# A one-element activation ahead of the second load in a cross-entropy kernel

## The chip, the cores and the metric

The kernel runs on one core of a Trainium2 chip. The metric is the device time of one execution in microseconds, lower is better. Before the change it is 85.4 us, the median of three runs (85.2 to 85.45).

## The reference

The input is `logits`, 256 rows of 32000 float32 (32.8 MB), and one label for each row. What is computed for each row is the cross-entropy with smoothed labels:

```python
log_probs = logits - np.max(logits, axis=-1, keepdims=True)
log_probs = log_probs - np.log(np.sum(np.exp(log_probs), axis=-1, keepdims=True))
smooth_targets = np.full((batch, num_classes), smoothing / num_classes)
for i, label in enumerate(labels):
    smooth_targets[i, label] = 1.0 - smoothing + smoothing / num_classes
return (-np.sum(smooth_targets * log_probs, axis=-1)).astype(np.float32)
```

Written out, a row's result is log(sum of exp(x)) minus c_small times (sum of x, plus c_big/c_small times x at the label), with c_small = smoothing / 32000 and c_big = 1 - smoothing. So each logit is read once, and goes into two sums: a sum of exponentials and a plain sum.

## The kernel before

**Layout.** The 256 rows lie as two rows (r = 0 and r = 1) on each of 128 partitions, so a partition has 64000 columns in a line, and the kernel walks along them in tiles. `WIDTHS` gives the tile widths. Row 0 has four tiles of 8000 columns. Row 1 has one of 8000, one of 6272, and then eight that become smaller: 4736, 3648, 2688, 2048, 1536, 1216, 1024 and 832.

**Buffers.** `load` (its transfers are at L166, L167 and L169 in the profile) takes the destination of a tile. Tiles of at least `RING_MIN` = 6000 columns, six in all, share a ring of three buffers and are called `xt` in the profile; a fourth can be loaded only when the first is no longer read. The eight smaller ones have a buffer each, in the pool `tail`, and are called `xl` in the profile. The names R0 to R5 and T2 to T9 in the prediction are these ring and tail tiles in the order of the columns.

**Work on a tile.** A tile is cut into pieces of at most 4032 columns: two for the six ring tiles and the first tail tile, one for the others. On each piece VectorE (DVE) adds its two halves and accumulates the sum (`sum_logits`, L175, output `jd`), and ScalarE (ACT) takes the exponential and accumulates it (`sum_exps`, L187, output `ja`). Both read the same tile, and neither needs the other.

**The rest.** GpSimd (POOL) loads the labels, computes flat indices and gathers the logit at each label (L103 to L123), and scales it into the first column of the plain sums (L146). When a row is complete, `finish` takes the logarithm of the exponential sum on ACT (L193 or L195), turns both results from a column into a row with two transposes on TensorE (L197, L201), and DVE combines them (L202). For row 1 the partial sums of the last tiles are added step by step in `done` (L268, L271, L276), so that little is left when the last tile has been read. One transfer writes the output (L280).

**What sets the order.** A scheduler, which works when the program is built, decides the order in which each engine and each queue issues, and it derives the waits from which instruction writes and which reads a tile. Within a queue or an engine, an instruction that waits holds up all that come after it. Every transfer of logits goes out on the queue of SyncE (SP), but for the second half of the first tile, which goes out on ACT's. The first transfers of both queues are then moved ahead of the program's opening barrier by `_issue_first_transfers_at_start`. ACT's table set (with Exp, Ln and Copy) is loaded once, at L90.

Of the kernel before, what the change touches and what calls it, by code (L numbers as in the profile page):

```python
# [8 lines left out]
FP32 = mybir.dt.float32  # L9
# [3 lines left out]
AF = mybir.ActivationFunctionType  # L13
# [3 lines left out]
WIDTHS = (  # L17
    (8000, 8000, 8000, 8000),
    (8000, 6272, 4736, 3648, 2688, 2048, 1536, 1216, 1024, 832),
)  # L20
# [37 lines left out]
def kernel(  # L58
# [7 lines left out]
    nc = tc.nc  # L66
    nc.at_finalize(_issue_first_transfers_at_start)
    B, C = logits.shape
    P = nc.NUM_PARTITIONS
# [12 lines left out]
    small = ctx.enter_context(tc.tile_pool(name="small", bufs=1))  # L82
# [6 lines left out]
    if tbl is not None:  # L89
        nc.scalar.add_instruction(  # L90
            mybir.InstLoadActFuncSet(
                name=nc.get_next_instruction_name(),
# [6 lines left out]

    x = logits.rearrange("(p r) c -> p (r c)", r=R)  # L100

    lab = small.tile([P, 2 * R], I32, name="lab", tag="lab")
    nc.gpsimd.dma_start(  # L103
        out=lab[:], in_=labels.bitcast(I32).rearrange("(p f) -> p f", p=P)
    )
    rowoff = small.tile([P, R], I32, name="rowoff", tag="rowoff")
    for r in range(R):
        nc.gpsimd.iota(
            out=rowoff[:, r : r + 1],
# [6 lines left out]
        out=flat_idx[:],  # L116
# [5 lines left out]
    for r in range(R):  # L122
        nc.gpsimd.indirect_dma_start(  # L123
            out=gat[:, r : r + 1],
            out_offset=None,
            in_=logits[:],
# [15 lines left out]
    for r in range(R):  # L142
# [4 lines left out]
            out=xsum[:, 0:1],  # L147
# [10 lines left out]
    def load(w: int, col: int, name: str):  # L158
        if w >= RING_MIN:
            xt = ring.tile([P, max(WIDTHS[0])], FP32, name="xt", tag="xt")  # L160
        else:
            xt = tail.tile([P, w], FP32, name=name, tag=name)
        if col == 0:

            h = w // 2
            nc.sync.dma_start(out=xt[:, :h], in_=x[:, :h])  # L166
            nc.scalar.dma_start(out=xt[:, h:w], in_=x[:, h:w])  # L167
        else:
            nc.sync.dma_start(out=xt[:, :w], in_=x[:, col : col + w])  # L169
        return xt  # L170
# [40 lines left out]
    col = 0  # L211
    for r in range(R - 1):
        at = 0
        for t, w in enumerate(WIDTHS[r]):
            xt = load(w, col, f"xl{r}_{t}")
            col += w
            k = pieces[r][t]
            for i in range(k):
                xp = xt[:, i * (w // k) : (i + 1) * (w // k)]
                sum_logits(xp, w // k, xsums[r][:, at + 1 : at + 2])  # L220
                sum_exps(xp, w // k, esums[r][:, at : at + 1])
                at += 1
        both = small.tile([P, 2], FP32, name=f"both{r}", tag=f"both{r}")
        nc.vector.tensor_reduce(  # L224
            out=both[:, 0:1], in_=xsums[r][:], axis=AX.X, op=ALU.add
        )
        nc.vector.tensor_reduce(  # L227
            out=both[:, 1:2], in_=esums[r][:], axis=AX.X, op=ALU.add
        )
        finish(r, both[:, 0:1], both[:, 1:2], None)  # L230
# [14 lines left out]
    for t, w in enumerate(WIDTHS[r]):  # L245
        left = n - 1 - t
        xt = load(w, col, f"xl{r}_{t}")
        col += w
        k = pieces[r][t]
# [16 lines left out]
        if left == 2:  # L266
            with tc.issue_after(part.ins):
                nc.vector.tensor_reduce(  # L268
                    out=done[0][:, 0:1], in_=xsum[:, : at + 1], axis=AX.X, op=ALU.add
                )  # L270
                nc.vector.tensor_reduce(  # L271
                    out=done[0][:, 1:2], in_=esum[:, : at - 1], axis=AX.X, op=ALU.add
                )
        elif left < 2:
            i = 1 - left
            nc.vector.tensor_tensor(  # L276
                out=done[i + 1][:], in0=done[i][:], in1=pairs[i][:], op=ALU.add
# [3 lines left out]
        out=out.rearrange("(g i) -> g i", g=1), in_=res[:].rearrange("g p r -> g (p r)")  # L281
# [36 lines left out]
```

The softmax here doesn't subtract the row's maximum and nothing guards it: scores larger than these inputs give would overflow.

## Time and profile before

| | before |
|---|---|
| median of three runs | 85.4 us |
| the profiled execution | 85.33 us |
| its span | 83.5 us |
| busy: ACT | 59.9 us (72%) |
| busy: DVE | 38.7 us (46%) |
| busy: POOL, PE | 4.2 and 1.5 us |
| moved by DMA | 32.78 MB, mean 392 GB/s |
| ACT idle before an `xt` tile | 19.3 us |
| DVE idle before an `xt` tile, an `xl` tile | 31.3 and 6.8 us |

The span runs from the first instruction of the program to the last one in the profile; the execution's time is 1.83 us more than that. The busy times are sums over stages that differ, so the stage has to be looked up before a number of this table is put to use. A transfer to the ring that is issued while others are queued takes a median of 21.6 us from issue to landing, most of it in the queue.

### The profile page before, as it was taken

Reading aid. Unit: us, or ns where it says so; the run is one execution under the profiler, and the core shown is the slowest. Engines: PE = TensorE matmul, PEld = TensorE weight load, DVE = VectorE, ACT = ScalarE, POOL = GpSimd, SP = SyncE. Lnnn points to the kernel's source line nnn. Section 1 sums busy time; section 2 is a strip of 40 time slices with the busy share of each in tenths; the row PEclk is TensorE's granted clock in tenths of the full one; section 3 lists DMA queues with packets and bytes.
Section 4 is the critical chain, followed back from the end, with each engine's and each line's share of the span. In section 5 each row is a group of like instructions: output and inputs, shape, how many; then the busy total and the mean of one; then the engine's idle time right before and its main releaser. Section 6 shows DMA issues by size and latency. Waiting matters only on the chain.

```text
span 83.5 us, 217 instructions
## 1 busy us (share of the span) xinstructions
PE 1.5 (2%) x4; PEld 0.3 (0%) x4; DVE 38.7 (46%) x52; ACT 59.9 (72%) x45; POOL 4.2 (5%) x14
## 2 busy tenths in 40 slices
PE   0000000000000000000001010000000000000030
PEld 0000000000000000000000000000000000000000
DVE  0000049600596009910497119913936654756660
ACT  5000049990599809993499909998999999999940
POOL 4201630011000000000000000000000000000000
DMA  5999998998899889998999899999999999999400
GB/s 130 421 422 429 421 506 368 491 460 383 383 490 490 383 352 490 490 398 352 475 490 414 352 419 480 456 396 426 426 392 433 418 422 415 409 411 410 182 4 0
DMA packets 2259, 32.78 MB, mean 392 GB/s; under 512 B 337, under 2 KB 338, under 8 KB 850
## 3 DMA queue, kind: packets, MB, share of 16 engines
q1 hardware_dynamic: 2018, 30.72, 87.0%
q10 hardware_dynamic: 144, 2.05, 5.7%
q0 software_dynamic: 96, 0.00, 0.1%
q14 instruction: 1, 0.01, 0.0%
HBM read 32.77 MB, written 0.00 MB: 392 GB/s over the span
## 4 chain that ended last, share of the span: by engine, by line
DMA 59%; ACT 34%; DVE 2%; issue 1%; PE 0%; SPq 0%; DVEq 0%; ACTq 0%
DMA xt<-in_logits_dram 59%; ACT ja L187 34%; DVE jd L175 1%; PE lin_t L197 0%; DVE done L276 0%; SPq L169 0%; DVE lin_row L199 0%; DVE res L202 0%; ACTq L187 0%; DVEq L202 0%; DVEq L276 0%
## 5 line engine op out<-in xcount | busy, mean ns | idle before, releaser
L187 ACT ACTIVATE ja<-xt 128x4000 bf16<-128x4000 f32 (+1 forms) x12 | 40.9, 3409 | 19.3 <-DMA xt<-in_logits_dram 19.3
L175 DVE SCALAR_TENSOR_TENSOR jd<-xt 128x2000 f32<-128x2000 f32 (+1 forms) x12 | 26.0, 2167 | 31.5 <-DMA xt<-in_logits_dram 31.3
L187 ACT ACTIVATE ja<-xl 128x2368 bf16<-128x2368 f32 (+7 forms) x9 | 16.5, 1839 | 0.0
L175 DVE SCALAR_TENSOR_TENSOR jd<-xl 128x1184 f32<-128x1184 f32 (+7 forms) x9 | 10.7, 1184 | 7.0 <-DMA xl<-in_logits_dram 6.8
L187 ACT ACTIVATION_READ_ACCUMULATOR ja<-xt 128x1 f32 x12 | 2.2, 187 | 0.0
L123 POOL DMA_INDIRECT gat<-in_logits_dram,flat_idx x2 | 2.0, 1002 | 0.7 <-POOL ident masks.py:199 0.4
L90 ACT ACT_TABLE_LOAD x1 | 1.3, 1283 | 0.9 <-PEq L299 0.9
L187 ACT ACTIVATION_READ_ACCUMULATOR ja<-xl 128x1 f32 x9 | 1.6, 182 | 0.0
L197 PE MATMUL lin_t<-ident,both 128*1 128x128 f32 x1 | 0.4, 371 | 45.6 <-DVE both L224 45.6
L175 DVE DVE_READ_ACCUMULATOR jd<-xt 128x1 f32 x12 | 1.0, 82 | 0.0
L199 DVE COPY lin_row<-lin_t 1x128 f32<-1x128 f32 x2 | 0.6, 278 | 0.9 <-PE lin_t L197 0.9
L197 PE MATMUL lin_t<-ident,done 128*1 128x128 f32 x1 | 0.4, 372 | 31.5 <-DVE done L276 31.5
L202 DVE SCALAR_TENSOR_TENSOR res<-lin_row,lse_t 1x128 f32<-1x128 f32 x2 | 0.6, 276 | 0.8 <-PE lse_t L201 0.7
L227 DVE TENSOR_REDUCE both<-esum 128x1 f32<-128x8 f32 x1 | 0.2, 164 | 1.6 <-ACT ja L187 1.6
L146 POOL TENSOR_SCALAR xsum<-gat 128x1 f32<-128x1 f32 x2 | 0.4, 222 | 7.9 <-DMA gat<-in_logits_dram,flat_idx 7.9
L103 POOL DMA_DIRECT2D lab<-in_labels_dram x1 | 0.8, 753 | 1.0 <-POOLq L299 1.0
L201 PE MATMUL lse_t<-ident,lse 128*1 128x128 f32 x2 | 0.7, 372 | 2.4 <-ACT lse L193 2.4
L175 DVE DVE_READ_ACCUMULATOR jd<-xl 128x1 f32 x9 | 0.7, 82 | 0.0
L276 DVE TENSOR_TENSOR done<-done,pair 128x2 f32<-128x2 f32 x2 | 0.3, 162 | 0.6 <-ACT ja L187 0.5
L115 POOL TENSOR_TENSOR flat_idx<-rowoff,lab 128x2 int32<-128x2 int32 x1 | 0.2, 195 | 5.4 <-DMA lab<-in_labels_dram 5.4
L195 ACT ACTIVATE lse<-elast,done 128x1 f32<-128x1 f32 x1 | 0.3, 261 | 0.2 <-DVE done L276 0.2
L193 ACT ACTIVATE lse<-both 128x1 f32<-128x1 f32 x1 | 0.2, 202 | 0.2 <-DVE both L227 0.2
(13 smaller groups left out, 2.0 us busy)
## 6 DMA issues: line engine op xcount, KB each, us to landing
xt<-in_logits_dram SPq DMA_DIRECT2D x4, 4000.0 KB, 21.6
xt<-in_logits_dram SPq DMA_DIRECT2D x1, 3136.0 KB, 19.2
xl<-in_logits_dram SPq DMA_DIRECT2D x1, 2368.0 KB
xt<-in_logits_dram SPq DMA_DIRECT2D x1, 2000.0 KB, 11.5
xt<-in_logits_dram ACTq DMA_DIRECT2D x1, 2000.0 KB, 13.1
xl<-in_logits_dram SPq DMA_DIRECT2D x1, 1824.0 KB, 28.3
xl<-in_logits_dram SPq DMA_DIRECT2D x1, 1344.0 KB, 31.1
xl<-in_logits_dram SPq DMA_DIRECT2D x1, 1024.0 KB, 33.1
```

What stands on the lines that cost most here:

```text
L90: nc.scalar.add_instruction(mybir.InstLoadActFuncSet(name=nc.get_next_instruction_name(), act_func_set_id=tbl, ins=[], outs=[],))
L103: nc.gpsimd.dma_start(out=lab[:], in_=labels.bitcast(I32).rearrange("(p f) -> p f", p=P))
L123: nc.gpsimd.indirect_dma_start(out=gat[:, r : r + 1], out_offset=None, in_=logits[:], in_offset=bass.IndirectOffsetOnAxis(ap=flat_idx[:, r ...
L146: nc.gpsimd.tensor_scalar(out=xsum[:, 0:1], in0=gat[:, r : r + 1], scalar1=label_weight, scalar2=None, op0=ALU.mult,)
L175: return nc.vector.scalar_tensor_tensor(out=jd[:, :h], in0=xp[:, :h], scalar=1.0, in1=xp[:, h:w], op0=ALU.mult, op1=ALU.add, accum_out=out,)
L187: nc.scalar.activation(out=ja[:, :w], in_=xp, func=AF.Exp, accum_out=out)
L195: nc.scalar.activation(out=lse[:], in_=se, func=AF.Ln, bias=se_rest)
L197: nc.tensor.transpose(out=lin_t[:], in_=lin, identity=ident[:])
L199: nc.vector.tensor_copy(out=lin_row[:], in_=lin_t[:])
L201: nc.tensor.transpose(out=lse_t[:], in_=lse[:], identity=ident[:])
L202: nc.vector.scalar_tensor_tensor(out=res[:, :, r : r + 1], in0=lin_row[:], scalar=-c_small, in1=lse_t[:], op0=ALU.mult, op1=ALU.add,)
L276: nc.vector.tensor_tensor(out=done[i + 1][:], in0=done[i][:], in1=pairs[i][:], op=ALU.add)
```

## The change

A tile `zero` of one column is set to 0 by DVE at the start. In `load`, ahead of the transfer of the second tile (`col == 8000`), ACT copies `zero` into the first column of that tile's buffer. The transfer then overwrites the column, so it has to wait for the copy; the copy stands behind the load of the tables on ACT. The transfer of the first tile, in two halves on two queues, is as it was. Nothing else in the source changes; line numbers after the edit are 3, and then 7, higher.

```diff
@@ -99,6 +99,9 @@
 
     x = logits.rearrange("(p r) c -> p (r c)", r=R)
 
+    zero = small.tile([P, 1], FP32, name="zero", tag="zero")
+    nc.vector.memset(zero[:], 0.0)
+
     lab = small.tile([P, 2 * R], I32, name="lab", tag="lab")
     nc.gpsimd.dma_start(
         out=lab[:], in_=labels.bitcast(I32).rearrange("(p f) -> p f", p=P)
@@ -160,6 +163,10 @@
             xt = ring.tile([P, max(WIDTHS[0])], FP32, name="xt", tag="xt")
         else:
             xt = tail.tile([P, w], FP32, name=name, tag=name)
+        if col == WIDTHS[0][0]:
+
+
+            nc.scalar.activation(out=xt[:, 0:1], in_=zero[:], func=AF.Copy)
         if col == 0:
 
             h = w // 2
```

## The prediction

> **What bounds the kernel now.** I read the slices of the page first, then the chain that ended last, then the instructions in order of time.
>
> ```profile
> DMA  5999998998899889998999899999999999999400
> DMA 59%; ACT 34%; DVE 2%; issue 1%; PE 0%; SPq 0%; DVEq 0%; ACTq 0%
> ```
>
> The first line is the share of the DMA engines in 40 slices of 2.09 us: full from the second to the 37th. The second is the chain by engine: DMA first, then ACT. The chain in order of time (start, us, what) says when it changes hands:
>
> ```profile
> 1.29 29.89 DMA xt<-in_logits_dram
> 31.27 7.16 ACT ja L187 x4
> 38.45 19.17 DMA xt<-in_logits_dram
> 57.70 5.60 ACT ja L187 x3
> 63.35 4.33 ACT ja L187 x3
> 67.72 3.19 ACT ja L187
> ```
>
> Until 57.7 us transfers set the time; ACT's 7.16 us on a ring tile sit on this chain only because a buffer's release starts the next transfer. From 57.70, when the last ring tile (6272 columns, call it R5) has landed, ACT runs without a hole to the end. The timeline (start, us, engine, line, operation; idle before it in brackets):
>
> ```profile
> 0.91 1.28 ACT L90 ACT_TABLE_LOAD   x1 [0.91 <-PEq L299]
> 0.92 1.09 SPq L169 DMA_DIRECT2D xt<-in_logits_dram  x2
> ...
> 11.50 3.54 ACT L187 ACTIVATE ja<-xt 128x4000 bf16<-128x4000 f32 x1 [9.31 <-DMA xt<-in_logits_dram]
> ...
> 21.73 3.54 ACT L187 ACTIVATE ja<-xt 128x4000 bf16<-128x4000 f32 x1 [3.07 <-DMA xt<-in_logits_dram]
> ...
> 57.70 2.82 ACT L187 ACTIVATE ja<-xt 128x3136 bf16<-128x3136 f32 x1 [0.31 <-DMA xt<-in_logits_dram]
> ...
> 63.36 1.39 DVE L175 SCALAR_TENSOR_TENSOR jd<-xl 128x1184 f32<-128x1184 f32 x1 [2.01 <-DMA xl<-in_logits_dram]
> ...
> 79.97 0.15 ACT L187 ACTIVATION_READ_ACCUMULATOR ja<-xl 128x1 f32 x1
> 80.06 0.16 DVE L276 TENSOR_TENSOR done<-done,pair 128x2 f32<-128x2 f32 x1
> ...
> 80.32 0.26 ACT L195 ACTIVATE lse<-elast,done 128x1 f32<-128x1 f32 x1 [0.20 <-DVE done L276]
> ...
> 81.38 0.32 SPq L280 DMA_DIRECT2D out_dram<-res  x1
> ```
>
> Two facts to take from these lines. From 57.70 to 80.12 (79.97 + 0.15) is 22.4 us of ACT work that cannot start earlier than R5. And the first tail tile (4736 columns, call it T2), next in the queue behind R5, lands at about 63.34, since DVE was waiting for it and started at 63.36.
>
> **What the Trainium skill says.** "DMA: Bandwidth & Descriptors", section "Queues, rings and completion order": on each DMA engine a queue's descriptors are consumed in ring order, though completion is not strictly first in, first out. The trace agrees on the order: two 4.1 MB transfers issued together at 0.92 let their readers go at 21.73 and 31.27, one after the other. "Specifications" of that page gives a fabric ceiling of 435 GB/s; the windows of this trace show 427 to 435 GB/s in the ring stage. "Perfetto Trace Analysis", section "Tensor Engine Instruction (MATMUL, LD_WEIGHTS)", calls ACT and DVE strict FIFO: ACT will not take a tile that has landed while an earlier instruction waits. Here ACT indeed sat 9.31, 3.07, 2.40, 2.33 and 1.91 us before ring tiles.
>
> **The change, part by part.** I compared the order in which both built programs issue. ACT, DVE and POOL keep the order of their tile work (two 128-row reductions of `done` move by a place near DVE's end); SP's queue does not:
>
> ```
> before  R0 first half | R1 R2 R3 R4 R5 T2 T3 ... T9 out
> after   R0 first half | T2 R1(waits for ACT) R2 R3 R4 R5 T3 ... T9 out
> ```
>
> (R0 to R5 are the ring tiles of 8000, 8000, 8000, 8000, 8000 and 6272 columns, T2 to T9 the tail; the second half of R0 goes from ACT's queue as before.) The new ACT copy writes into R1, so R1's transfer now has a writer to wait for. T2 has a buffer of its own and waits for nothing, and the scheduler puts it into the free place. So the second transfer issued is not held at all; it is a tile that is wanted only after all six ring tiles.
>
> *Memset on DVE (128x1).* Nearest row: 0.16 us (the 128x1 reductions). DVE is idle until 11.50. Zero; uncovered, 0.16.
>
> *Copy on ACT (128x1).* Nearest row: the 128x1 ACTIVATE of L193, 0.20 us. ACT is idle from 2.19 to 11.50 waiting for R0. "ScalarE: Activation LUTs", section "What ACT_TABLE_LOAD costs", gives about 1.28 us for the load (the trace: 1.28) plus about 1.38 us of drain, which this trace does not show. So the copy ends between 2.19 + 0.2 + 0.1 = 2.5 and 3.9 us. Queued behind it on ACT is R0's first exponential, waiting until 11.50 anyway. Zero; uncovered, 0.2 to 1.7.
>
> *The hold on R1.* Behind it on SP wait R2 to R5, T3 to T9 and the output. R1 is issued at 2.5 to 3.9 us instead of 0.92. At that time the queues hold R0 (4.1 MB) and T2 (2.42 MB). R0 and R1 before let the reader go at 21.73; T2 has 3264 columns fewer than R1, 1.67 MB or 3.9 us at 430 GB/s, so R0 and T2 keep the DMA engines busy until some 17.8 us, less what lies between the last byte and the landing, which the trace does not split off. The hold has a margin of 12 us or so. Zero; from about 15 us on it would cost 1 us for each.
>
> *T2 ahead of R1 to R5.* 128 x 4736 x 4 bytes = 2.425 MB, carried before all ring tiles but the first. The price can be read without a rate: after the change R5 ends at the same count of bytes at which T2 ended before, so it lands when T2 landed: 63.34 instead of 57.66, **+5.68 us**. With the rate of the ring stage (431 GB/s) it is 2.425 / 0.431 = 5.63. I take 5.66. Does a ring buffer starve on the way? R3 waits for R0's buffer (18.68, unchanged; T2 and R1, R2 are in the queue until about 37). R4 waits for R1's, free at 21.73 + 5.66 + 7.1 = 34.5, with R2 and R3 queued until 46.4; R5 is issued at 44 with R3, R4 queued until 56. The queue never runs dry, so the shift neither grows nor shrinks.
>
> ACT does not use the early T2: its instruction stays behind R5's two. So ACT waits 5.66 us longer for R1, then again follows the transfers at 9.5 us a tile, with 7.2 us of work each, and begins its 22.4 us on R5 at 57.70 + 5.66 = 63.36. Before, those 22.4 us lay beside the tail's transfers with almost no slack on either side; now T3 to T9 land at their old times (67.7 to 79.0, same byte counts) while ACT needs T3 only at 73.4. The cover is lost on the transfer side and nothing is gained on ACT's.
>
> *What comes back at the end.* ACT and DVE now never wait for the tail. Between tiles ACT's steps from one accumulator read to the next start are 0.09 to 0.16 us in the tail against 0.09 within a tile, 0.23 more in all: between 0 and 0.23 comes back, I take 0.1. And the last logarithm at 80.32 waited for DVE's `done` (80.06 + 0.16), which hung on the late sum of T9; now DVE is ahead, and it can start some 0.06 after ACT's end at 80.12: 0.12 comes back. The transposes and the output (2.1 us from 81.38) stay.
>
> *Semaphores of SP.* T5 waits for T2's landing, T8, T9 and the output now wait for the landing of R3, R4 and R5 (before: T7, T8, T9 for R3, R4, R5). T9 goes out by about 56, when over 20 us of transfers are queued. Zero.
>
> **Sum**: 5.66 - 0.10 - 0.12 = +5.44. Span 83.5 + 5.44 = 88.9; the profiled execution's 85.33 becomes 90.77. The median of the runs, 85.4, lies 0.07 above that execution, so 90.8.
>
> **Rivals.**
>
> *The early T2 costs nothing, time stays at 85.4.* This needs R5 to land by 57.7 although 2.425 MB more lie ahead of it: the DMA engines would have to carry 26.1 MB (51008 columns) instead of 23.7 in the 56.4 us from 1.29, 463 instead of 420 GB/s on average. Single slices of the page show 490 and 506, but each has a neighbour at 352 to 383; over whole tiles the windows give 427 to 435, at the page's ceiling. It decides from about 460 GB/s on. Chance 2%, and in it a lucky version that is faster: under 1%.
>
> *The issue order is not what fixes the order of landing*: packets of T2 and of the ring tiles are mixed so that T2 is served last. Then R1 lands at 21.7, the copy and hold are hidden and the time is 85.3 to 85.5. It speaks against it that the ring tiles landed strictly in the order issued. 2%.
>
> *The hold is long.* If the wait of R1 lasted past some 15 us, transfers would stop, and every us would come on top: 92 and more. The table load ended at 2.19 and nothing behind it waits for data. 2%.
>
> *ACT gains back more.* If ACT's steps shorten once the transfers are over (its last 5 us now run beside none), the increase could be 4.9 instead of 5.4: 90.2. The 4000-column exponentials last 3.52 to 3.54 us throughout, which speaks against more than some tenths. This lies in the main case's spread.
>
> **How the numbers follow.** Main case, slower by 5.4: 94%. Its own spread: 5.63 to 5.68 on the transfers, 0 to 0.35 back at the end, some 0.25 of scatter between runs (85.2 to 85.45) and the rate's own: 90.1 to 91.4. The other cases hold 6% and need not be reached. Slower: main case and long hold, 96%; same (within 0.3%, about what this kernel's measurement can tell): 3%; faster 1%.
>
> **What would show it.** In the profile after: SP's first issue past the barrier is a transfer to `xl`; ACT's second ring tile starts at about 27.4 instead of 21.7, and its idle time for `xt` grows from 19.3 to about 25; the first 3136-column exponential starts near 63.4; DVE's waits for `xl` (6.8 us) vanish, DMA slices are full to the same 78 us, and then ACT runs alone for about 6 us. The step on the hold is wrong if the DMA slices show a hole before 17 us; the step on R5 is wrong if it starts much off 63.4; the end is wrong if ACT's stretch from R5 to the last accumulator read is not 22.2 to 22.4 us.

## The result and the profile after

The changed kernel takes 90.38 us (median of six runs, 90.26 to 90.91) against 85.39 us before (six runs, 85.2 to 85.56). The ratio is 1.0594, with a 95% interval of 1.0565 to 1.0623: slower by 4.99 us. The prediction was 90.8, with 90.1 to 91.4 as its range.

The timeline of the kernel after (start, us, engine, line, operation; in brackets the idle time before it and what ended it), at the places that were shown of before:

```profile
0.91 1.28 ACT L90 ACT_TABLE_LOAD   x1 [0.91 <-PEq L306]
0.92 0.33 SPq L176 DMA_DIRECT2D xl<-in_logits_dram  x1
...
2.21 0.20 ACT L169 ACTIVATE xt<-zero 128x1 f32<-128x1 f32 x1
...
2.44 41.91 SPq L176 DMA_DIRECT2D xt<-in_logits_dram  x5
...
11.41 3.54 ACT L194 ACTIVATE ja<-xt 128x4000 bf16<-128x4000 f32 x1 [9.00 <-DMA xt<-in_logits_dram]
...
27.36 3.54 ACT L194 ACTIVATE ja<-xt 128x4000 bf16<-128x4000 f32 x1 [8.80 <-DMA xt<-in_logits_dram]
...
63.28 2.82 ACT L194 ACTIVATE ja<-xt 128x3136 bf16<-128x3136 f32 x1 [0.31 <-DMA xt<-in_logits_dram]
...
68.89 2.16 ACT L194 ACTIVATE ja<-xl 128x2368 bf16<-128x2368 f32 x1
...
85.25 0.15 ACT L194 ACTIVATION_READ_ACCUMULATOR ja<-xl 128x1 f32 x1
85.43 0.26 ACT L202 ACTIVATE lse<-elast,done 128x1 f32<-128x1 f32 x1
...
86.46 0.32 SPq L287 DMA_DIRECT2D out_dram<-res  x1
```

The first transfer past the barrier is one to `xl`, T2, issued at 0.92 and held by nothing. R1 goes out at 2.44, as soon as the copy is done. ACT's second tile starts at 27.36, which was 21.73 before, and R5 at 63.28, which was 57.70. From there ACT again works without a hole up to the last logarithm. T2 took 16.9 us from issue to landing, by the page's list of DMA issues (KB, us), so it lay ready from 17.8 us on. ACT, idle for 8.80 us until 27.36, took it only at 68.89, behind R5:

```profile
xl<-in_logits_dram SPq DMA_DIRECT2D x1, 2368.0 KB, 16.9
```

The windows of the kernel after (stretch, length, then the busy time of PE, PEld, DVE, ACT and POOL, the clock, the DMA share and GB/s) show what has become of the overlap at the end:

```profile
63.30:69.00 5.70, 0.00 (x0) 0.00 (x0) 5.60 (x7) 5.70 (x5) 0.00 (x0) 1.00 0.99 421
69.00:78.00 9.00, 0.00 (x0) 0.00 (x0) 7.59 (x14) 9.00 (x7) 0.00 (x0) 1.00 1.00 410
78.00:86.00 8.00, 0.63 (x2) 0.16 (x2) 1.97 (x8) 7.66 (x13) 0.00 (x0) 1.00 0.04 14
```

The windows of the kernel before, at the same end:

```profile
63.40:78.00 14.60, 0.00 (x0) 0.00 (x0) 9.63 (x16) 14.60 (x15) 0.00 (x0) 1.00 1.00 416
78.00:81.00 3.00, 0.72 (x2) 0.16 (x2) 1.81 (x7) 2.38 (x7) 0.00 (x0) 1.00 0.09 34
```

Transfers run to about 78 us at 410 to 421 GB/s, as before (416). Then they are over, and ACT still has 7.66 us of work where it had 2.38 before: the difference lay beside transfers before. The waits, in total, turn round in the same way:

```profile
ACT ja L194 <- DMA xt<-in_logits_dram: 24.7, 6, 9.0
DVE jd L182 <- DMA xl<-in_logits_dram: 1.1, 2, 0.6
```

ACT's wait for ring tiles was 19.3 us and is now 24.7; DVE's for tail tiles was 6.8 and is now 1.1. One view of this profile misleads. The page's chain by engine reads:

```profile
DMA 72%; ACT 14%; issue 8%; SPq 2%; PE 0%; DVE 0%; ACTq 0%
```

That looks as if transfers bound the kernel more than before (59%). But from 63.28 on ACT is the bound, as the windows show. The same chain in order of time (start, us, what) shows where it goes astray:

```profile
45.81 29.36 DMA xl<-in_logits_dram
...
75.21 1.14 issue
76.35 0.38 ACT ja L194 x2
76.73 2.05 issue
```

It steps from ACT to the landing of a tail tile that ACT had not been waiting for, and books a part of ACT's exponentials as "issue". A chain is to be checked against the busy time of the stage.

### The profile page after: what moved, and what is told of

Its sections match the earlier page's. It is cut to its first block, busy times and chain, and to the rows that moved or that the text cites. A ratio compares the mean times of both kernels' runs of the same rounds, so it can differ in the third digit from the quotient of the medians.

```text
span 88.5 us, 221 instructions
## 1 busy us (share of the span) xinstructions
PE 1.5 (2%) x4; PEld 0.3 (0%) x4; DVE 38.9 (44%) x53; ACT 59.8 (68%) x46; POOL 4.3 (5%) x14
## 4 chain that ended last, share of the span: by engine, by line
DMA 72%; ACT 14%; issue 8%; SPq 2%; PE 0%; DVE 0%; ACTq 0%
DMA xt<-in_logits_dram 38%; DMA xl<-in_logits_dram 33%; ACT ja L194 12%; SPq L176 2%; ACT L90 1%; PE lse_t L208 0%; DVE res L209 0%; ACT lse L202 0%; ACT xt L169 0%; ACTq L194 0%
## 5 line engine op out<-in xcount | busy, mean ns | idle before, releaser
L194 ACT ACTIVATE ja<-xt 128x4000 bf16<-128x4000 f32 (+1 forms) x12 | 40.9, 3409 | 24.7 <-DMA xt<-in_logits_dram 24.7
L194 ACT ACTIVATE ja<-xl 128x2368 bf16<-128x2368 f32 (+7 forms) x9 | 16.4, 1829 | 0.0
## 6 DMA issues: line engine op xcount, KB each, us to landing
xl<-in_logits_dram SPq DMA_DIRECT2D x1, 2368.0 KB, 16.9
```

The lines of the kernel that those rows point to most:

```text
L194: nc.scalar.activation(out=ja[:, :w], in_=xp, func=AF.Exp, accum_out=out)
```

## The experiments

Theory O: what costs is the order, T2's bytes ahead of five ring tiles while ACT's instruction for T2 stays behind them, and the hold is covered by what is queued. Rival H: the hold, the copy or the memset cost the time. The table sums up all runs; the second column is when SP's queue issued R1, the third when ACT started R5, the fourth from there to the start of the last logarithm. The times are medians; of the kernel before the median was 85.28 to 85.39 beside each.

| kernel | R1 issued | R5 on ACT | from R5 to the last log | time, us | ratio to before, 95% |
|---|---|---|---|---|---|
| before | 0.92 | 57.70 | 22.62 | 85.39 | |
| after | 2.44 | 63.28 | 22.15 | 90.38 | 1.0565 to 1.0623 |
| hold, tail in place | 2.44 | 57.58 | 22.44 | 84.99 | 0.9954 to 0.9978 |
| T2 first, no hold | 1.30 | 63.28 | 22.15 | 90.46 | 1.0591 to 1.0624 |
| T2 first and used early | 2.44 | 63.36 | 17.83 | 86.09 | 1.0079 to 1.0109 |
| T5 first, no hold | 1.30 | 60.14 | 22.26 | 87.32 | 1.0227 to 1.0261 |
| T2 and T3 first, no hold | 2.16 | 67.65 | 22.15 | 94.81 | 1.1095 to 1.1138 |
| T2 first, hold to 16 | 16.08 | 63.97 | 22.14 | 90.93 | 1.0638 to 1.0707 |
| T2 first, hold to 19 | 18.65 | 66.76 | 22.14 | 93.73 | 1.0956 to 1.1001 |
| hold to 19, tail in place | 18.83 | 66.78 | 22.44 | 93.96 | 1.0984 to 1.1030 |
| memset only | 0.92 | 57.64 | 22.45 | 85.08 | 0.9965 to 0.9983 |
| memset and copy, no hold | 0.92 | 57.74 | 22.45 | 85.02 | 0.9953 to 0.9973 |
| hold, tail in place, again | 2.44 | 57.77 | 22.44 | 85.00 | 0.9950 to 0.9975 |

### The hold without the order

The changed kernel, with each transfer on SP's queue tied behind the one before it in the source (an edge for the order of issue, with no wait), so that T2 goes back to its place.

```diff
-            nc.sync.dma_start(out=xt[:, :w], in_=x[:, col : col + w])
+            if last_load:
+                with tc.issue_after(last_load[-1].ins):
+                    d = nc.sync.dma_start(out=xt[:, :w], in_=x[:, col : col + w])
+            else:
+                d = nc.sync.dma_start(out=xt[:, :w], in_=x[:, col : col + w])
+            last_load.append(d)
```

> The memset, the copy on ACT and the hold on R1 are kept; the transfers on SP's queue are put back into the order of the columns (R1 to R5, then T2 to T9). Theory O (the order costs, the hold is covered): the hold until 2.44 us lies under R0's 4.1 MB, which keep the DMA engines busy until about 11 us, so R5 starts on ACT at 57.7 again and the time is that of before, 85.4 within 0.3%. Rival H (the wait, the copy or the memset cost something of their own): above 86, up to the 90.4 of the changed kernel.

Measured: 84.99 us. SP's queue and the start of R5 in the timeline of this kernel:

```profile
2.44 0.33 SPq L182 DMA_DIRECT2D xt<-in_logits_dram  x1
...
57.58 2.82 ACT L201 ACTIVATE ja<-xt 128x3136 bf16<-128x3136 f32 x1 [0.30 <-DMA xt<-in_logits_dram]
```

R1 is held until 2.44 as in the changed kernel, and R5 starts at 57.58. The hold, the memset and the copy cost nothing; the whole loss has gone with the order. The time is even 0.34% below that of before (0.22 to 0.46%), which theory O did not expect; the last experiment follows that up.

### The order without the hold

The kernel before, with T2's transfer issued ahead of R1's; the edges of the first experiment, left out below, keep this order on SP's queue. There is no memset, copy or hold.

```diff
+            if t == 1:
+                for e in EARLY:  # (2,)
+                    ahead[e] = load(
+                        WIDTHS[1][e], WIDTHS_0 + sum(WIDTHS[1][:e]), f"xl1_{e}"
+                    )
             xt = load(w, col, f"xl{r}_{t}")
```

> The kernel before, without memset, copy or hold; only T2's transfer is issued ahead of R1's. Theory O: all of the loss, 90.4 (90.2 to 90.6), R5 on ACT at 63.3. Rival H: 85.4, or at most a part of the 5 us.

Measured: 90.46 us. SP's queue and the start of R5 in the timeline of this kernel:

```profile
0.92 0.33 SPq L177 DMA_DIRECT2D xl<-in_logits_dram  x1
1.30 43.06 SPq L175 DMA_DIRECT2D xt<-in_logits_dram  x5
...
63.28 2.82 ACT L196 ACTIVATE ja<-xt 128x3136 bf16<-128x3136 f32 x1 [0.30 <-DMA xt<-in_logits_dram]
```

R1 leaves at 1.30 instead of 2.44, and R5 starts at 63.28 all the same. The order makes all of the loss, and the two runs together decide for theory O.

### T2 first, and used when it lands

The changed kernel with the hold; DVE's and ACT's work on T2 is put right behind that on R0. The edges, and the lines that skip T2 at its old place, are left out below; `load(...)` is shortened.

```diff
+            if t == 0:
+                for e in EARLY:  # (2,)
+                    ahead[e] = load(...)
+                    k, c = pieces[1][e], sum(pieces[1][:e])
+                    h = WIDTHS[1][e] // k
+                    for i in range(k):
+                        xp = ahead[e][:, i * h : (i + 1) * h]
+                        sum_logits(xp, h, xsums[1][:, c + i + 1 : c + i + 2])
+                        sum_exps(xp, h, esums[1][:, c + i : c + i + 1])
```

> The changed kernel (hold kept, T2 first), but the sums and exponentials of T2 stand right behind R0's on DVE and ACT instead of behind R5's. Theory O with ACT in order: R5 still lands at 63.3, but ACT's 4.33 us on T2 now lie between 18.5 and 27.4, where it had been idle for 8.8 us; from R5 on it has 22.12 - 4.33 = 17.8 us of work and no wait for T3 to T9 (each lands before its turn), so it ends at 81.1 and the execution takes 85.39 + 0.7 = 86.1. Rival T (what costs is that the ring tiles land late, whatever ACT does meanwhile): 90.4, as in the changed kernel.

Measured: 86.09 us. ACT in the timeline of this kernel:

```profile
18.52 2.16 ACT L203 ACTIVATE ja<-xl 128x2368 bf16<-128x2368 f32 x1
...
20.68 2.16 ACT L203 ACTIVATE ja<-xl 128x2368 bf16<-128x2368 f32 x1
...
27.44 3.54 ACT L203 ACTIVATE ja<-xt 128x4000 bf16<-128x4000 f32 x1 [4.50 <-DMA xt<-in_logits_dram]
...
63.36 2.82 ACT L203 ACTIVATE ja<-xt 128x3136 bf16<-128x3136 f32 x1 [0.31 <-DMA xt<-in_logits_dram]
...
81.19 0.26 ACT L211 ACTIVATE lse<-elast,done 128x1 f32<-128x1 f32 x1
```

R5 is as late as in the changed kernel, at 63.36, and yet 4.29 us of the loss are back. ACT did T2's 4.33 us in a wait before R1, which shrank from 8.80 to 4.50, and they are gone from the stretch after R5 (17.83 us instead of 22.15). What is left over before, 0.8 us (86.09 against 85.29 beside it), is the lateness that this doesn't make up: R5 starts 5.66 us later, and the stretch after it is 4.79 us shorter. So most of the cost isn't that the ring tiles are late, but that the work for the early bytes stays behind them in ACT's order.

### More or fewer bytes ahead

The kernel before with other tail tiles ahead of R1, again without a hold: T5 alone (`EARLY = (5,)`), then T2 and T3 (`EARLY = (2, 3)`), in the manner of the second experiment.

> The kernel before without a hold, with a smaller tail tile, T5 (2048 columns, 1.05 MB), ahead of R1. Theory O: the shift is that of the bytes, 1.049 MB / 0.431 MB per us = 2.43 us, less the 0.45 us that came back at the end in the changed kernel: 87.4. Rival S (what costs is one transfer out of order, not its bytes): 90.4.

> The kernel before without a hold, with T2 and T3 (8384 columns, 4.29 MB) ahead of R1. Theory O: the bytes give 4.293 / 0.431 = 9.96 us, less 0.45: 94.9, R5 on ACT at 67.7. Rival (the cost levels off, since the ring's three buffers or ACT's spare time take up a part of a longer delay): below 94.

Measured: 87.32 and 94.81 us. The start of R5 with T5 ahead, and with T2 and T3 ahead:

```profile
60.14 2.82 ACT L196 ACTIVATE ja<-xt 128x3136 bf16<-128x3136 f32 x1 [0.30 <-DMA xt<-in_logits_dram]
```

```profile
67.65 2.82 ACT L196 ACTIVATE ja<-xt 128x3136 bf16<-128x3136 f32 x1 [0.30 <-DMA xt<-in_logits_dram]
```

Against 57.70 the shifts are 2.44, 5.58 (T2) and 9.95 us for 1.049, 2.425 and 4.293 MB: 0.430, 0.435 and 0.431 MB per us. R5's delay is that of the bytes, in a straight line from 1 to 4 MB, whether one or two transfers carry them. The whole time grows by 0.4 to 0.5 us less (by 2.03, 5.17 and 9.47 us), because the stretch after R5 is shorter than before, as the table shows.

### How long a hold is covered

T2 first, by the edges of the first two experiments. In one kernel the copy into R1 is made by DVE behind both of R0's sums, in another by ACT behind both of R0's exponentials; a third has the latter hold with the tail in its place. The edit of the second:

```diff
-            nc.scalar.activation(out=xt[:, 0:1], in_=zero[:], func=AF.Copy)
+            with tc.issue_after(exps[-1].ins):  # R0's second exponential
+                nc.scalar.activation(out=xt[:, 0:1], in_=zero[:], func=AF.Copy)
```

> T2 first and the hold on R1 made longer: the copy is made by DVE behind both of R0's sums, so R1 is issued at about 16.2 us instead of 2.44. The prediction put the point from which the hold costs at about 15 us. R0 and T2 are 6.5 MB; at 0.27 MB until 2.1 us and 0.43 MB per us from there they last until 16.7, and from an issue to the first byte some 1.1 us pass (the first issue at 0.0 and the half-filled first DMA slice), so a hole of about 0.6 us: 91.0 (90.5 to 91.4). If the hold is not covered by what is queued, the cost is 13.8 us: over 100.

> T2 first and the hold longer still: ACT's copy stands behind R0's two exponentials, R1 is issued at about 18.8 us. The queue is dry from 16.7 to about 19.9: a hole of 3.2 us in the DMA slices, R5 on ACT at 66.5, 93.6 (93.2 to 94.0).

> The same long hold (R1 at about 18.8 us) with the tail in its place, so only R0's 4.1 MB are queued, which last until about 11.0. A hole of 8.9 us: 94.3 (93.7 to 94.7), 0.7 above the kernel with the same hold and T2 first although no byte is out of order: then T2 is worth as cover what it costs as order. Rival (a hold costs the same whatever is queued): 3.2 us above before, 88.6.

Measured: 90.93, 93.73 and 93.96 us. Of each, SP's issue of R1 and the start of R5. T2 first, the hold to 16:

```profile
16.08 28.95 SPq L185 DMA_DIRECT2D xt<-in_logits_dram  x5
...
63.97 2.82 ACT L208 ACTIVATE ja<-xt 128x3136 bf16<-128x3136 f32 x1 [0.31 <-DMA xt<-in_logits_dram]
```

T2 first, the hold to 19:

```profile
18.65 29.12 SPq L185 DMA_DIRECT2D xt<-in_logits_dram  x5
...
66.76 2.82 ACT L207 ACTIVATE ja<-xt 128x3136 bf16<-128x3136 f32 x1 [0.30 <-DMA xt<-in_logits_dram]
```

The hold to 19 with the tail in place, with the DMA share of its page (40 slices of 2.31 us) ahead:

```profile
DMA  7899800078999999999999999899999999999800
...
18.83 0.33 SPq L185 DMA_DIRECT2D xt<-in_logits_dram  x1
...
66.78 2.82 ACT L205 ACTIVATE ja<-xt 128x3136 bf16<-128x3136 f32 x1 [0.30 <-DMA xt<-in_logits_dram]
```

If each further us of hold delays R5 by one us, the time of issue less the delay of R5 is the moment up to which a hold is free. (Between the two holds with T2 first, 2.57 us of hold cost 2.79.) With R0 and T2 queued the delays against 63.28 are 0.69 and 3.48: free up to 16.08 - 0.69 = 15.4 and 18.65 - 3.48 = 15.2 us. With R0 alone the delay against 57.70 is 9.08: free up to 9.75 us. The two differ by 5.5 us, T2's bytes once more. With R0 alone there was one hold only, so its 9.75 rests on that one-to-one price. The zeros in the slices are the hole itself. SP issued nothing between 0.40 and 18.83 us, though T2 to T9 did not depend on the copy: within its queue the held R1 kept all of them back. The hold to 19 costs about the same with and without T2 in front (66.76 and 66.78): there T2 fills a hole that the hold had torn. The two totals differ by 0.23 us and not by the expected 0.7. The expectation for the tail in place was 0.3 too high, mostly because it started from 85.4; with the memset in the kernel that base is 85.0.

### Why the hold alone is a little faster than before

Three kernels, measured on one chip: the memset alone, the memset and ACT's copy into a tile of its own, and the hold with the tail in place again.

```diff
+    zero = small.tile([P, 1], FP32, name="zero", tag="zero")
+    nc.vector.memset(zero[:], 0.0)
+
+    spare = small.tile([P, 1], FP32, name="spare", tag="spare")  # second kernel only
+    nc.scalar.activation(out=spare[:], in_=zero[:], func=AF.Copy)
```

> Why is the kernel with the hold and the tail in place 0.3 us faster than before? Its profile shows two parts: R5 starts 0.12 us sooner, and the first step of `done` no longer sits 0.52 us idle behind the sum of T8, so the last logarithm starts 0.17 us sooner after ACT's end. This kernel is the kernel before with the memset alone: no copy, no hold. Theory D (one more instruction on DVE's list removes the idle time before `done`, whatever its cause; nothing to do with the hold): 85.1, no idle time before the first step of `done`. Theory X (the hold on R1 itself gains): 85.3, as before.

> The kernel before with the memset and with ACT's copy into a tile of its own: both instructions of the change, no hold. Theory D: 85.1. Theory X: 85.3. If the copy and not the memset brings the gain: 85.0 here and 85.3 with the memset alone.

> The kernel with the hold and the tail in place once more, so that it stands beside the two others on the same chip: 85.0 if the gain is there at all; 85.3 if it was that chip's. Theory X says it is 0.3 below the two others, theory D at most 0.15.

Measured: 85.08, 85.02 and 85.00 us, with 85.28 for before; the intervals of the three ratios overlap, and the hold adds nothing to the memset that can be told. So the gain is not the hold's: theory D. The second kernel shows one thing more: with both new instructions, but no dependence of R1 on the copy, R1 goes out at 0.92 and T2 stays in its place. It is the dependence that moved T2. The timeline of DVE before, and then with the memset alone:

```profile
78.69 0.08 DVE L175 DVE_READ_ACCUMULATOR jd<-xl 128x1 f32 x1
79.29 0.16 DVE L276 TENSOR_TENSOR done<-done,pair 128x2 f32<-128x2 f32 x1 [0.52 <-ACT ja L187]
79.36 0.58 DVE L175 SCALAR_TENSOR_TENSOR jd<-xl 128x416 f32<-128x416 f32 x1
```

```profile
78.63 0.08 DVE L178 DVE_READ_ACCUMULATOR jd<-xl 128x1 f32 x1
78.81 0.16 DVE L279 TENSOR_TENSOR done<-done,pair 128x2 f32<-128x2 f32 x1
79.02 0.59 DVE L178 SCALAR_TENSOR_TENSOR jd<-xl 128x416 f32<-128x416 f32 x1
```

With the memset DVE's 0.52 us of idle time ahead of `done` are gone, and the last logarithm starts 0.03 us after ACT's end instead of 0.20. Why they were there is open. `done` needs T7's exponential there, and T7's accumulator had been read by 78.16; the waits written into both programs for these steps are the same but for the count that the memset shifts by one. What the trace shows is when the idle time ended: `done` started at 79.29, just when ACT had read the accumulator of T8, one tile later (79.09 + 0.19), although the program doesn't ask for it. With the memset `done` started at 78.81, ahead of that. The supposed 0.12 us at R5 is none: the three kernels start it at 57.64, 57.74 and 57.77, around the 57.70 of before. These three kernels are 0.26 to 0.37% faster than the kernel before; none that moved a tail tile or held R1 longer was.

## Why the prediction was right

**The order of issue.** Right, and the step that decides. It came from comparing what the two built programs issue, not from the source: there the change touches R1 alone, and it is T2 that moves.

**T2's bytes.** Foretold was +5.66 us on R5, measured +5.58. Reading the shift off the old landing of T2 (5.68) was about as good as the rate (5.63), and the runs with T5 and with T2 and T3 bear out both.

**ACT in order.** Foretold: ACT waits, does not use T2, and then carries its whole stretch alone. The run with T2 used early shows it by removing it: 4.29 us come back.

**What comes back at the end.** The mechanism was right, the sizes too small. From R5 to the last accumulator read ACT took 22.12 us instead of 22.42: 0.30 came back, where 0.10 was taken and 0.23 was the upper end. Some 0.21 of it is gaps, nearly all that there were to lose; 0.09 is shorter exponentials on the tail tiles (nine of 1829 ns instead of 1839), which was not foreseen. The logarithm's wait gave 0.17 instead of 0.12; by the prediction's own figures (80.32 against 80.12 + 0.06) that term should have been 0.14. The order alone removes this wait (22.15 us from R5 to the logarithm without memset or hold, too), and so does the memset alone: the wait hung on the late sum of T9, as the prediction says, but the idle time before the first step of `done` had made that sum late. So 5.58 - 0.30 - 0.17 = 5.11 against 5.44; the two profiled executions differ by 4.93 (90.26 and 85.33), since 0.03 more came back in the last operations and 0.15 from the issue of the output to the end of the execution. Of the forecast's excess of 0.51 (5.44 against 4.93), then, 0.25 lies in the two terms of the end, 0.08 in R5's shift, and 0.18 behind the logarithm, where the prediction had left all as it was; why that part became shorter is open.

**The hold, the copy, the memset at nothing.** Right for the hold: free up to some 15 us with T2 queued, as worked out, and up to 9.75 without. Of the copy's two bounds, 2.5 and 3.9 us, the lower one held: it started at 2.21, 0.02 us after the table load ended. For the memset it was right in this change, where the stretch after R5 is 22.15 us with and without it; in the kernel before, with the tail in place, it brings 0.2 us.

**The rivals.** That the early T2 costs nothing would have needed 463 GB/s; R5's shift shows 435. One argument against it was read too neatly: not every slice of 490 GB/s has a neighbour at 352 to 383 (one lies between 475 and 414). Landing followed the order of issue: in the kernel after, T2 had landed by 17.8 us, and ACT started the ring tiles behind it at 27.36, 36.84, 46.33, 55.82 and 63.28. The long hold did not occur in this change; where an edge made it long, it cost what was priced. "ACT gains back more" came nearest to the time: it said 4.9, and 4.99 was measured. But ACT's steps account for only 0.2 us of that, and they were shorter while transfers still ran: T2's first exponential took 2.16 us at 68.89, 2.18 before. So its reason, that no transfers run beside, isn't what the trace shows.

**What should show.** Nearly all did: 27.36, 63.28, 24.7 us of waits. DVE's waits for `xl` fell to 1.1 us and did not vanish, and ACT's stretch was 22.12 us, just outside 22.2 to 22.4: by the prediction's own sign its step on the end was wrong in size.

## What to carry to other kernels

A dependence that is put on one transfer can do more than hold that transfer: here the scheduler filled the place with a tile that waited for nothing, and the price was that tile's bytes in front of the consumers that were next in line. Compare the issued order of both programs before pricing a wait, and fix the order by edges if only the wait is meant. Early bytes were worth something here only when the engine that uses them could do so early (86.09 against 90.38 us). And where transfers and compute end almost together, as in the kernel before, there is little slack to absorb a shift. What T2 costs ahead of fewer ring tiles, R5 alone for instance, was not tried.

## What was not expected

One memset at the start of DVE's list, whose result nothing reads, made the kernel before 0.2 us faster (ratio 0.9974, 0.9965 to 0.9983). With it 0.52 us of idle time near the end of the same engine's list are gone. Why is open. Whoever compares kernels at 0.3% has to reckon with such shifts from instructions that do nothing for the work itself.

After the table load there was no further pause: the copy started 0.02 us after the load's end. The Trainium skill, "ScalarE: Activation LUTs", section "What ACT_TABLE_LOAD costs", counts about 1.38 us of drain beside the load's 1.28 for every switch to a different set. The load here is the only one of the program, so no run shows such a switch; the prediction's upper bound for the copy, 3.9 us, rested on a cost that didn't arise.
